# Moving copy-outs, head steps and one row fetch in the mixer stage of a hybrid diffusion layer

## The chip, the core and the metric

The kernel runs on one core of a Trainium2 chip. The core has a matrix engine (TensorE, in the profile PE, with its weight loads as PEld), a vector engine (VectorE, DVE), a scalar engine (ScalarE, ACT), GpSimd (POOL) and a queue engine (SyncE, SP) that here only issues transfers. Each works through its own list of instructions in the order in which the program left them, and waits for the others by semaphores. Sixteen DMA engines, shared by all queues, move data between main memory and the on-chip buffers. The metric is the device time of one execution in microseconds (us), lower is better.

## The reference

One layer of a diffusion backbone over 256 latent and 256 context tokens, D_MODEL = 2048, in float32. What matters here:

```python
qa, ka, va, qb, kb, vb, rb, lrf, lrb, gate_a, gate_b = jnp.split(h @ w_in, offs, axis=-1)
gf = log_sigmoid(lrf @ w_gate_f + b_gate_f) / GLA_GATE_NORM        # and gb, per GLA head
...
o_attn = windowed_attention(qa, ka, va, cka, cva, attn_sink)
o_gla = latent_gla(qb, kb, vb, gf, gb, sf, sb)                     # 4 heads, two directions
y_att = o_attn @ w_attn_o
y_gla = (rms_norm(o_gla, gla_norm) * silu(rb)) @ w_gla_o
x = x + mod_x[2] * ((sigmoid(gate_a) * y_att + sigmoid(gate_b) * y_gla) @ w_out)
x = x + mod_x[5] * conv_ffn(modulate(x, ...), w_up, conv_w, conv_b, w_down)
```

`gate_a` and `gate_b` are two products of the normalised latent tokens with 2048 columns of `w_in` each. The four heads of the gated linear attention (GLA) need, for each head, a decay computed from low-rank columns and then a 256 x 256 matrix built up in eight levels of doubling block size.

## The kernel before

Every large product streams a float32 weight in tiles of 256 rows by 512 columns (512 KB). A tile is loaded by SP into a buffer called `raw` (line 105, a pool `wr` of seven, which the copies to memory and the token rows share), ACT rounds it to `whi` (line 220), DVE subtracts to get `wlo` (line 221), both in pools of three, and PE multiplies both with the high and low halves of the activations `h..hi`, `h..lo` into banks `acc` (line 84; four banks). Splits are put ahead of other work of their engine where the scheduler can.

`proj_nat` and `proj_T` run such a product for 512 columns over eight tiles. Ahead of each tile they call `tick()`, and in its middle `midway()`; both advance whatever runs beside the product:

- `later`: functions handed to `defer(n, fn)`, called n ticks later;
- `beside = [generator, rate, 0.0]`: `aside()` adds the rate at every tick and every midway and takes one step of the generator per whole unit;
- `bg_steps` and `bg_rate`: one background step per whole unit at each tick. Each step (`mod_latent`) loads 512 KB of `w_modT` into a `raw` buffer and runs one custom DVE instruction on it (line 403). There are 100 steps, to be used up before the output product.

The stage of interest comes after the first products. Blocks in order: KB (`kb_block`, keys of heads 2 and 3, latent and context tokens, eight tiles of 24 matmuls), KA (`kept(KA, ...)`, the same size), then eight gate blocks `gate_blocks` of 512 columns for the latent tokens only: GA0 to GA3 and GB0 to GB3, eight tiles of 12 matmuls each. Then `all_values` runs 17 steps of `inner` (line 84, banks `pg`) and `outer`.

`kept` copies the finished banks to a `raw` buffer on ACT (line 1010) and sends it to memory by a DMA issued from ACT's own queue (line 1012), to be read again much later. `evac` is called as soon as the block's matmuls have been written down.

Beside these blocks run the four GLA heads, one generator `along()` of 16 places per head. `gate(h)` makes one of four pieces of the decay (matmul `pz`, ACT, DVE, POOL), `gla_A` is the levels: per level up to four exponentials on ACT (lines 892, 893, 899, 900), two products on DVE (894, 901), up to four additions on DVE on `segs` (903 to 906), eight small matmuls `pa` (line 96), a predicated copy (875); then the end of a head (lines 917 to 921, splits by lines 62 and 63, and the last `pa` products). `with_gla` gives head 0 to KB and head 1 to KA at rate 1.0 (16 calls of `aside`, 16 places), head 2 to GA0-GA3 and head 3 to GB0-GB3 at rate 0.3 (64 calls each); what is left of a head when its blocks are written down is run at once.

In GB3 the rows of the context and latent tokens are fetched again: `fetch(step)` loads, for two steps at a time, 1 MB `rows` (a broadcast of `drows`) and for each step 512 KB of `x` and `ctx` into a `raw` buffer; `natural(step)` scales, splits and writes them to memory (`dh`) and then fetches the next step. `fetch(0)` comes at GB3's first tick, `natural(0)` two and `natural(1)` five ticks later. A `rows` tile takes a large buffer of pool `M` (16 buffers) that something else has to leave first.

Of the kernel before, what the change touches and what calls it, by code (L numbers as in the profile page):

```python
# [32 lines left out]
def layer_kernel(ctx, tc, A, out):  # L33
# [115 lines left out]
    def defer(n, fn):  # L149

        later.append([n, fn])
# [808 lines left out]
            gates[h] = next(it), it  # L960
        next(gates[h][1])

    def with_gla(h, kb, block, rate=1.0):
        own = []

        def level():
            if not own:
                own.append(gla_A(h, kb, qbt, *gates[h][0]))
            next(own[0], None)

        this, following = lambda: gate(h), lambda: gate(h + 1)
        places = {i: [this] for i in ((0, 1, 2, 3) if h == 0 else (0, 1))}
        for i in (4, 6, 7, 8, 9, 10, 11, 12) if h == 0 else (2, 4, 5, 7, 8, 10, 11, 12):
            places[i] = [level]
        places.update({13: [level], 14: [following], 15: [level]})
        places.setdefault(13 if h == 0 else 9, []).append(following)

        def along():
            for i in range(16):
                for fn in places.get(i, ()):  # L980
                    fn()
                yield

        beside[:] = [along(), rate, 0.0]
        v = block()
        for _ in beside[0]:
            pass
        beside.clear()
        return v

    def kb_block():
        kb = []

        def evac(i, b):
            if not kb:
                kb.append(M("kb1", [P, 4, 512]))
            S.activation(kb[0][:, i, :], b, AF.Copy)

        proj_T(w_in, KB + 512, ALL, [h_both], evac, by_tile=True)
        return kb[0]  # L1000

    def kept(c0, name, lhs, by_tile=False):
        n = len(lhs)
        d = dram.tile([P, n, 512], F32, name=name)
        raw = []

        def evac(i, b):
            if i % 2 == 0:
                raw[:] = [wr.tile([P, 2, 512], F32, name="raw", tag="raw")]
            S.activation(raw[0][:, i % 2, :], b, AF.Copy)  # L1010
            if i % 2:
                nc.scalar.dma_start(d[:, i - 1:i + 1, :], raw[0])

        proj_nat(w_in, 0, c0, ALL, lhs, evac, by_tile=by_tile)
        return d
# [4 lines left out]
    def fetch(step):  # L1020
        if step >= KT:
            return
        kp = step % (KT // 2)
        raw = wr.tile([P, 4, T], F32, name="raw", tag="raw")
        if step >= KT // 2:
            load(raw, dh[kp])
            fetched[step] = raw
            return
        if kp % 2 == 0:
            r = M("rows", [P, 2, 4, T])  # L1030
            load(r, drows[kp:kp + 2].rearrange("k r d -> (k r d)").partition_broadcast(P))
            rows[step], rows[step + 1] = r[:, 0], r[:, 1]
        for s, src in enumerate((A["x"], A["ctx"])):
            load(raw[:, 2 * s:2 * s + 2, :], src[0][:, kp * T:(kp + 1) * T].rearrange("(t p) d -> p t d", p=P))
        fetched[step] = raw

    defer(2, send_rows)
    kb1 = with_gla(0, kbt, kb_block)
    dka = with_gla(1, kbt, lambda: kept(KA, "dka", h_xc, True))
    gate_a, gate_b = [], []  # L1040

    def gate_blocks(c0, name, to):
        for j in range(4):
            if c0 == GB and j == 3:
                defer(0, lambda: fetch(0))
                defer(2, lambda: natural(0))
                defer(5, lambda: natural(1))
            to.append(kept(c0 + j * 512, f"{name}{j}", h_x))

    def natural(step):  # L1050
        raw = fetched.pop(step)
        e = step % 2
        if step >= KT // 2:
            a = S.activation(hh[e][:, 1], raw, AF.Copy).ins
            in_order(last_hi[0], a)
            in_order(last[0], a)
            a = V.tensor_tensor(hl[e][:, 1], raw, hh[e][:, 1].bitcast(F32), op=ALU.subtract).ins
            in_order(last_lo[0], a)
            fetch(step + 1)
            return  # L1060
        r = rows.pop(step)
        for i in range(4):
            a = V.scalar_tensor_tensor(raw[:, i, :], raw[:, i, :], rcol[:, i:i + 1], r[:, i // 2, :],
                                       op0=ALU.mult, op1=ALU.mult).ins
            in_order(last_lo[0], a)
            in_order(last[0], a)
        for s in range(2):
            x_ = raw[:, 2 * s:2 * s + 2, :]
            V.tensor_tensor(x_, x_, r[:, 2 + s:3 + s, :].to_broadcast([P, 2, T]), op=ALU.add)
        split(hh[e][:, 1], hl[e][:, 1], raw)  # L1070
        nc.scalar.dma_start(dh[step], raw)
        fetch(step + 1)

    bg_rate[:] = [0.3, 0.0]
    with_gla(2, kb1, lambda: gate_blocks(GA, "da", gate_a), 0.3)
    with_gla(3, kb1, lambda: gate_blocks(GB, "db", gate_b), 0.3)
    bg_rate[:] = [0.0, 0.0]

    att = M("att", [P, 2048])
# [65 lines left out]
    def all_values():  # L1145
        last_kp = KT // 2 - 1
        banks = []

        def inner(step):
            e = step % 2  # L1150
            ax, ac = pair_x[step // (KT // 2)], pair_c[step // (KT // 2)]
            hn = (hh[e][:, 1], hl[e][:, 1])
            gb = [bank("pg", (P, 2, T), side=True) for _ in range(2)]
            for n, (x_, y_) in enumerate(((0, 0), (0, 1), (1, 0))):
                for k in range(2):
                    for s in range(4):
                        if s < 2:
                            m_ = ax[:, y_, :, 2 * s:2 * s + 2, :].rearrange("p h b c -> p h (b c)")
                        else:
                            m_ = ac[:, y_, :, s - 2, :]  # L1160
                        mm(gb[k], hn[x_][:, s, k * P:(k + 1) * P], m_, start=(n == 0 and s == 0),
                           stop=(n == 2 and s == 3))
            for k in range(2):
                split(hh[2 + e][:, 1, 2 * k:2 * k + 2, :], hl[2 + e][:, 1, 2 * k:2 * k + 2, :], gb[k])

        def outer(step, i, w):
            kp, pair, e = step % (KT // 2), step // (KT // 2), step % 2
            if kp + i == 0:
                banks[:] = [acc.tile([P, 512], F32, name="acc", tag="acc") for _ in range(4)]
            hi, lo = w  # L1170
            gs = [g[2 + e][:, 1].rearrange("p (k h) t -> p k h t", h=2) for g in (hh, hl)]

            def part0(t):
                for k in range(2):
                    for x_ in range(2):
                        mm(banks[2 * i + t], gs[x_][:, k, i, t * P:(t + 1) * P], hi[:, k, :],
                           start=(kp == 0 and k + x_ == 0), stop=False)

            def part1(t):
                for k in range(2):  # L1180
                    mm(banks[2 * i + t], gs[0][:, k, i, t * P:(t + 1) * P], lo[:, k, :], start=False,
                       stop=(kp == last_kp and k == 1))

            if kp == last_kp:
                for t in range(2):
                    part0(t)
                    part1(t)
                    out_pair(pair, i, t, banks[2 * i + t])
                return
            for part in (part0, part1):  # L1190
                for t in range(2):
                    part(t)

        def out_pair(pair, i, t, po):
            if len(og) <= pair:
                og.append(M("og", [P, 2, 2, 512]))
            S.activation(og[pair][:, i, t, :], po, AF.Copy)
            junk = W2("fb", "junk", [P, 512])
            S.activation(junk, po, AF.Square, accum_out=ssg[:, 2 * pair + i, t:t + 1])

        for step in range(KT + 1):
            if step in (1, KT // 2):
                bg_rate[:] = [0.3 if step == 1 else 0.7, 0.0]
            if 0 < step < KT - 1:
                natural(step + 1)
            if step < KT:
                inner(step)
            if step:
                pair, kp = divmod(step - 1, KT // 2)
                for i in range(2):  # L1210
                    tick()
                    c0 = VB + (2 * pair + i) * 512
                    outer(step - 1, i, wsplit(w_in[kp * 2 * P:(kp + 1) * 2 * P, c0:c0 + 512]))
# [134 lines left out]
            pass  # L1348
        beside.clear()

    bg_rate[0] = 0.75
    for j in range(1, 4):
        rb_block(j)

# [276 lines left out]
```

## Time and profile before

| what | value |
|---|---|
| median of three runs | 1969.03 us (1967.55 to 1970.83) |
| the profiled execution | 1970.05 us, its span 1968.3 us |
| KB and KA | 197.8 to 315.7 us of the span |
| GA0 to GA3 | 315.7 to 429.8 us |
| GB0 to GB3 | 429.8 to 544.8 us |
| all_values | 544.8 to about 711 us |

The block boundaries are the starts of the first matmul of a block in the timeline of PE. Times inside the profile count from the start of the span; 1.75 us of the profiled execution lie around it. "Busy" counts instructions in work; the idle time in front of a group is put down to what ended it (the releaser). A row of the stretches view gives, for a stretch, the busy time of each engine with its instruction count, then the clock granted to PE, the share of time that the DMA engines were busy, and GB/s.

### The profile page before, as it was taken

To read this page: it belongs to the slowest core of one execution; us is meant where nothing else is said; L and a number is where in the kernel's file an instruction comes from. 1 tells how busy PE (TensorE), PEld (TensorE's weight loads), DVE (VectorE), ACT (ScalarE), POOL (GpSimd) and SP (SyncE) were. 2 spreads that over 40 slices of the span, in tenths; PEclk is the share of its full clock that TensorE was granted. 3 is DMA by queue.
4 is the path that set the end of the run, shared out by engine and by line. 5 is a ranking of instruction groups with operands and counts; after the bars stand their busy time and mean duration, and the time that the engine had idled before them with its cause. 6 is when DMAs were issued, how large, how long until landed. Compare 5 with 4: busy or idle time off the path is not lost.

```text
span 1968.3 us, 26419 instructions
## 1 busy us (share of the span) xinstructions
PE 1928.2 (98%) x9858; PEld 1599.9 (81%) x9858; DVE 1446.6 (73%) x2241; ACT 1007.6 (51%) x1469; POOL 49.6 (3%) x81
## 2 busy tenths in 40 slices
PE   8999999999899999999999999999999999999999
PEld 6678787777688888778888888888888888888887
DVE  5756776858677858889888867898886545777754
ACT  5223666555344455666444445765555334555533
POOL 0010110000100000000000000000000000000000
PEclk9999999999999999999999999999999999999999
DMA  9984323757786765446999988688886566666663
GB/s 396 412 303 130 98 62 132 233 204 243 239 279 214 231 221 149 119 141 198 317 378 365 338 290 274 192 276 280 265 285 225 192 195 185 191 191 190 194 211 113
DMA packets 193376, 450.24 MB, mean 229 GB/s; under 512 B 13648, under 2 KB 18000, under 8 KB 187360
## 3 DMA queue, kind: packets, MB, share of 16 engines
q1 hardware_dynamic: 187568, 428.13, 65.3%
q0 software_dynamic: 2912, 10.82, 1.6%
q10 hardware_dynamic: 2768, 9.61, 1.2%
q8 instruction: 77, 1.26, 0.3%
q14 instruction: 51, 0.42, 0.1%
HBM read 435.86 MB, written 12.65 MB: 228 GB/s over the span
## 4 chain that ended last, share of the span: by engine, by line
PE 92%; DMA 4%; DVE 2%; ACT 1%; issue 0%; ACTq 0%; SPq 0%; DVEq 0%
PE acc L84 68%; PE accs L84 12%; PE pg L84 4%; PE pa L96 2%; DMA raw<-in_w_in 2%; PE poa L96 1%; PE pS L96 1%; DMA mraw<-in_w_mod 1%; PE pm L96 1%; PE ptp L99 1%; DMA xr<-in_ctxT 1%; DVE wlo L221 1%; ACT whi L220 1%; ACT raw L1010 0%; DMA db<-raw 0%
## 5 line engine op out<-in xcount | busy, mean ns | idle before, releaser
L221 DVE TENSOR_TENSOR wlo<-raw,whi 128x1024 fp32r<-128x1024 f32 x568 | 692.5, 1224 | 365.5 <-ACT whi L220 355.4
L220 ACT ACTIVATE whi<-raw 128x1024 fp32r<-128x1024 f32 x568 | 600.0, 1060 | 700.4 <-PE acc L84 416.8
L84 PE MATMUL accs<-h,whi 128*128 128x512 f32 x704 | 244.5, 392 | 0.0
L84 PE MATMUL acc<-h,whi 128*128 128x512 f32 x640 | 222.3, 392 | 0.0
L84 PE MATMUL accs<-h,wlo 128*128 128x256 f32 x704 | 196.0, 278 | 0.0
L84 PE MATMUL acc<-h,wlo 128*128 128x256 f32 x640 | 178.1, 278 | 0.0
L84 PEld LDWEIGHTS accs<-h,whi 128*128 128x128 f32 x704 | 131.8, 187 | 29.9
L84 PEld LDWEIGHTS acc<-h,whi 128*128 128x128 f32 x640 | 119.8, 187 | 27.0
L84 PE MATMUL acc<-whi,ah 128*128 128x512 f32 x352 | 137.0, 389 | 0.0
L84 PE MATMUL acc<-whi,al 128*128 128x512 f32 x352 | 137.0, 389 | 0.0
L84 PEld LDWEIGHTS accs<-h,wlo 128*128 128x128 f32 x704 | 132.5, 188 | 0.0
L84 PEld LDWEIGHTS acc<-h,wlo 128*128 128x128 f32 x640 | 120.5, 188 | 0.1
L84 PE MATMUL acc<-whi,h0hi 128*128 128x512 f32 x192 | 79.3, 413 | 23.0 <-ACT whi L220 23.0
L84 PE MATMUL acc<-whi,h2hi 128*128 128x512 f32 x256 | 101.5, 396 | 0.0
L84 PE MATMUL acc<-whi,h3hi 128*128 128x512 f32 x256 | 100.5, 393 | 0.8 <-ACT whi L220 0.8
L84 PE MATMUL acc<-whi,th 128*128 128x512 f32 x256 | 100.5, 393 | 0.0
L84 PE MATMUL acc<-whi,h3lo 128*128 128x512 f32 x256 | 99.8, 390 | 0.0
L84 PE MATMUL acc<-whi,h2lo 128*128 128x512 f32 x256 | 99.8, 390 | 0.0
L84 PE MATMUL acc<-whi,tl 128*128 128x512 f32 x256 | 99.7, 389 | 0.0
L84 PE MATMUL acc<-wlo,ah 128*128 128x512 f32 x352 | 94.2, 389 | 0.0
L403 DVE CUSTOM_DVE_ANT_0 raw<-raw,csrow,pack 128x1024 f32<-128x1024 f32 x64 | 81.8, 1279 | 0.0
L84 PE MATMUL acc<-whi,h0lo 128*128 128x512 f32 x192 | 78.0, 406 | 0.0
(389 smaller groups left out, 3589.1 us busy)
## 6 DMA issues: line engine op xcount, KB each, us to landing
raw<-in_w_in SPq DMA_DIRECT2D x204, 512.0 KB, 4.5
raw<-in_w_up SPq DMA_DIRECT2D x176, 512.0 KB, 4.5
raw<-in_w_modT SPq DMA_DIRECT2D x128, 512.0 KB, 5.0
raw<-in_w_down SPq DMA_DIRECT2D x88, 512.0 KB, 4.0
mraw<-in_w_mod SPq DMA_DIRECT2D x32, 1024.0 KB, 13.9
raw<-in_w_attn_o SPq DMA_DIRECT2D x32, 512.0 KB, 5.7
raw<-in_w_gla_o SPq DMA_DIRECT2D x32, 512.0 KB, 6.0
raw<-in_w_out SPq DMA_DIRECT2D x32, 512.0 KB, 5.9
```

What stands on the lines that cost most here:

```text
L84: r = pe_seq(PE.matmul(*a, **k))
L96: return pe_seq(after(PE.matmul(*a, **k)))
L99: return pe_seq(after(PE.transpose(*a)))
L220: j = S.activation(hi[:, 0:n, :], raw[:, 0:n, :], AF.Copy).ins
L221: i = V.tensor_tensor(lo[:, 0:n, :], raw[:, 0:n, :], hi[:, 0:n, :].bitcast(F32), op=ALU.subtract).ins
L403: i0 = V.tensor_tensor_reduce(out=raws[i], in0=raws[i], in1=row[0], scale=1.0, scalar=d if h else bmod[:, b0:b0 + 1], op0=ALU.mult, op1=AL ...
```

## The change

- `kept.evac`: for blocks with two banks (all gate blocks, not KA) the two copies and the DMA are deferred by two ticks, into the next block, or into `all_values` for GB3.
- The four heads become one generator `all_heads` of 64 places. It runs at 0.85 in KB and KA and at 0.32 in all gate blocks, without being emptied between blocks.
- `natural(1)` no longer fetches step 2; `all_values` does so at its start.
- The background rate is 0.35 for 0.3 in the gate blocks, 0.4 for 0.3 in the first half of `all_values`, 0.72 for 0.75 in the last products before the merge.

```diff
+    kbs = [kbt, kbt]
-    def with_gla(h, kb, block, rate=1.0):
+    def head_steps(h):
         own = []
         def level():
             if not own:
-                own.append(gla_A(h, kb, qbt, *gates[h][0]))
+                own.append(gla_A(h, kbs[h], qbt, *gates[h][0]))
             next(own[0], None)
...
-        def along():
-            for i in range(16):
-                for fn in places.get(i, ()):
-                    fn()
-                yield
-
-        beside[:] = [along(), rate, 0.0]
-        v = block()
-        for _ in beside[0]:
-            pass
-        beside.clear()
-        return v
+        for i in range(16):
+            for fn in places.get(i, ()):
+                fn()
+            yield
+
+    def all_heads():
+        for h in range(4):
+            yield from head_steps(h)
...
-        def evac(i, b):
+        def copy_out(i, b):
             if i % 2 == 0:
                 raw[:] = [wr.tile([P, 2, 512], F32, name="raw", tag="raw")]
             S.activation(raw[0][:, i % 2, :], b, AF.Copy)
             if i % 2:
                 nc.scalar.dma_start(d[:, i - 1:i + 1, :], raw[0])
+
+        def evac(i, b):
+            if n > 2:
+                copy_out(i, b)
+            else:
+                defer(2, lambda: copy_out(i, b))
...
-    kb1 = with_gla(0, kbt, kb_block)
-    dka = with_gla(1, kbt, lambda: kept(KA, "dka", h_xc, True))
+    beside[:] = [all_heads(), 0.85, 0.0]
+    kbs.extend([kb_block()] * 2)
+    dka = kept(KA, "dka", h_xc, True)
...
-        fetch(step + 1)
-    bg_rate[:] = [0.3, 0.0]
-    with_gla(2, kb1, lambda: gate_blocks(GA, "da", gate_a), 0.3)
-    with_gla(3, kb1, lambda: gate_blocks(GB, "db", gate_b), 0.3)
+        if step != 1:
+            fetch(step + 1)
+    bg_rate[:] = [0.35, 0.0]
+    beside[1] = 0.32
+    gate_blocks(GA, "da", gate_a)
+    gate_blocks(GB, "db", gate_b)
+    for _ in beside[0]:
+        pass
+    beside.clear()
...
+        fetch(2)
         for step in range(KT + 1):
             if step in (1, KT // 2):
-                bg_rate[:] = [0.3 if step == 1 else 0.7, 0.0]
+                bg_rate[:] = [0.4 if step == 1 else 0.7, 0.0]
...
-    bg_rate[0] = 0.75
+    bg_rate[0] = 0.72
```

How the change moves instructions, at two places. First ACT, where block GA0 ends and GA1 begins; `whi<-raw` is the split of a weight tile, `raw<-acc` the copy-out of the two banks, `da<-raw` its DMA, the others belong to a head. Before, the rows from the last exponential of GA0 on; the three splits at the end are GA1's first three tiles:

```order
L893 ACTIVATE q_3109<-segs 128x64x4
L1010 ACTIVATE raw<-acc 128x512 x2
L1012 DMA da_2859<-raw 128x1024
L899 ACTIVATE k_3113<-segs 128x64x4
L900 ACTIVATE k_3113<-segs 128x64x4
L220 ACTIVATE whi<-raw 128x1024 x3
```

In the changed kernel the first split row here is that of GA1's second tile (its first stands some rows further up), and the last one that of GA1's third tile:

```order
L220 ACTIVATE whi<-raw 128x1024
L817 ACTIVATE ge<-ge,ones 128x512
L892 ACTIVATE q_3126<-segs 128x256
L892 ACTIVATE q_3191<-segs 128x128x2
L62 ACTIVATE ac<-pa 128x512
L899 ACTIVATE k_3195<-segs 128x128x2
L1007 ACTIVATE raw<-acc 128x512 x2
L892 ACTIVATE q_3245<-segs 128x64x4
L1009 DMA da_2758<-raw 128x1024
L220 ACTIVATE whi<-raw 128x1024
```

The copies and their DMA moved behind the splits of the next block's first two tiles; ahead of the third split stand now the copies, the DMA and one exponential. At the other five boundaries from GA1 to GB3 the copies stand in the same way between the second and the third split.

Second SP, the loads around the start of GB3. `in_w_in` are weight tiles, `in_w_modT` background loads, `rows<-drows` a row fetch, `in_x` and `in_ctx` the tokens. Before, the first row of three weight tiles is the middle of GB2, the second its last three, and the row of two is GB3's first two; the row fetch is that of steps 2 and 3, the tokens are those of steps 0 and 1:

```order
L105 DMA raw<-in_w_in 128x2x512 x3
L105 DMA raw<-in_w_modT 128x1024
L105 DMA raw<-in_w_in 128x2x512 x3
L105 DMA rows<-drows 128x2048
L105 DMA raw<-in_x 128x2x256
L105 DMA raw<-in_ctx 128x2x256
L105 DMA raw<-in_w_modT 128x1024
L105 DMA raw<-in_w_in 128x2x512 x2
L105 DMA raw<-in_x 128x2x256
L105 DMA raw<-in_ctx 128x2x256
```

After, the first row is GB2's last two tiles, the two single weight tiles are GB3's first and second, the row of two at the end its third and fourth; the row fetch is again that of steps 2 and 3:

```order
L105 DMA raw<-in_w_in 128x2x512 x2
L105 DMA raw<-in_x 128x2x256
L105 DMA raw<-in_ctx 128x2x256
L105 DMA raw<-in_w_in 128x2x512
L105 DMA raw<-in_w_modT 128x1024
L105 DMA raw<-in_w_in 128x2x512
L105 DMA rows<-drows 128x2048
L105 DMA raw<-in_x 128x2x256
L105 DMA raw<-in_ctx 128x2x256
L105 DMA raw<-in_w_in 128x2x512 x2
```

The row fetch moved behind GB3's first two weight tiles and the tokens of step 0. The buffer that it waits for is another one too: before it was the `segs` of head 3, read last by line 920; now it is the buffer of the queries `qb`, read last by line 921 of the same head, one DVE instruction later. The tokens of step 2 moved from behind GB3's fifth weight tile to behind its eighth.

## The prediction

> **What bounds the kernel now.** I read the page's busy totals first, then PE's waits in the stage that changes, then that stage cut at the block boundaries.
>
> ```profile
> PE 1928.2 (98%) x9858; PEld 1599.9 (81%) x9858; DVE 1446.6 (73%) x2241; ACT 1007.6 (51%) x1469; POOL 49.6 (3%) x81
> ```
>
> PE is the bound, and nothing here takes products away from it. What can be won is idle time of PE and time in which it runs slowly. The waits of PE in the gate blocks (315 to 545 us: engine and line, what it waited for, us in total, times, longest):
>
> ```profile
> PE acc L84 <- ACT whi L220: 23.8, 9, 8.3
> PE acc L84 <- DVE wlo L221: 0.4, 1, 0.4
> ```
>
> Nearly all is one wait, for ACT's split. Seven of its nine times are the starts of GA0 to GB2, some 2 us each, one, of 8.25 us, is the start of GB3, and the ninth, 0.82 us, lies within GB3. The stretches of the eight blocks follow (us; PE, PEld, DVE, ACT, POOL busy with counts; granted clock; DMA share; GB/s):
>
> ```profile
> 315.74:343.50 27.76, 25.88 (x114) 21.42 (x114) 17.81 (x26) 15.81 (x25) 2.15 (x2) 0.94 0.60 202
> 343.50:370.46 26.96, 24.77 (x120) 20.63 (x120) 24.84 (x44) 14.36 (x26) 0.00 (x0) 1.00 0.70 225
> 370.46:400.17 29.71, 27.53 (x129) 22.85 (x129) 20.40 (x32) 16.17 (x27) 1.00 (x1) 0.94 0.59 195
> 400.17:429.77 29.60, 27.36 (x113) 22.34 (x113) 15.19 (x19) 13.62 (x20) 0.97 (x1) 0.94 0.59 197
> 429.77:455.98 26.21, 24.31 (x114) 20.26 (x114) 21.21 (x32) 15.83 (x25) 2.86 (x3) 1.00 0.82 299
> 455.98:483.66 27.68, 25.07 (x120) 20.55 (x120) 23.65 (x42) 14.92 (x26) 0.00 (x0) 1.00 0.62 200
> 483.66:517.60 33.94, 25.68 (x128) 21.52 (x128) 23.43 (x37) 16.17 (x26) 4.08 (x11) 0.95 0.63 214
> 517.60:544.80 27.20, 26.37 (x120) 21.80 (x121) 21.01 (x29) 9.93 (x10) 3.49 (x5) 0.94 0.87 289
> sum 229.06, PE 206.97 PEld 171.37 DVE 167.54 ACT 116.82 POOL 14.55; mean PE 25.87 PEld 21.42 DVE 20.94 ACT 14.60 POOL 1.82
> ```
>
> The stage lasts 229.06 us. How short could it be? Pieces of the chain of waits give the price of each kind of PE work (start, us, engine and line, count):
>
> ```profile
> 556.52 5.44 PE acc L84 x24
> 495.76 0.89 PE pa L96 x8
> 305.02 0.23 PE pz L96
> 251.92 3.45 PE pa L96 x16
> 307.97 2.87 PE pa L96 x24
> ```
>
> A weight matmul undisturbed takes 5.44 / 24 = 0.227 us, so 8 blocks x 8 tiles x 12 = 768 of them take 174.1 us. Two heads have 7 levels with 8 small products each beyond the first, and four more groups: I count 144 at 0.89 / 8 = 0.111 us, 16.0 us; six `pz` at 0.23, 1.4 us; and the ends of heads 2 and 3, priced like those of heads 0 and 1, 3.45 and 2.87 us. That is 197.8 us. **The excess is 229.1 - 197.8 = 31.3 us**, the most that the eight blocks can give.
>
> Where does it lie? First the idle time: 23.8 + 0.4, less the 2.15 before GA0 that stand ahead of the stretch, is 22.1 us. A boundary looks like this on PE and on ACT (start, us, instruction, in brackets the idle time before it):
>
> ```profile
> 315.74 0.63 PE L84 MATMUL acc<-whi,h0hi 128*128 128x512 f32 x1 [2.15 <-ACT whi L220]
> 370.48 0.73 PE L84 MATMUL acc<-whi,h0hi 128*128 128x512 f32 x1 [2.18 <-ACT whi L220]
> 517.61 0.80 PE L84 MATMUL acc<-whi,h0hi 128*128 128x512 f32 x1 [8.25 <-ACT whi L220]
> 367.88 1.08 ACT L1010 ACTIVATE raw<-acc 128x512 f32<-128x512 f32 x2 [0.94 <-PE acc L84]
> 369.00 0.33 ACTq L1012 DMA_DIRECT2D da<-raw  x1
> 369.37 2.95 ACT L220 ACTIVATE whi<-raw 128x1024 fp32r<-128x1024 f32 x3 [0.40 <-ACT raw L1010]
> ```
>
> ACT stands in order: it waits for the block's last matmul, copies (1.08), issues the DMA (0.33), and only then splits the next block's first tile (2.95 / 3 = 0.98). That is the wait of 2.18 us.
>
> Second, slow clock. In five of the eight rows the granted clock is 0.94 or 0.95. In GB2's the low clock falls into the idle 8.25 us at its end; for three others the chain shows what it costs:
>
> ```profile
> 370.48 3.68 PE acc L84 x8
> 315.74 6.40 PE acc L84 x20
> 400.19 4.58 PE acc L84 x12
> ```
>
> Eight matmuls behind the wait take 3.68 instead of 8 x 0.227 = 1.81 us, 1.87 more; 6.40 for 20 and 4.58 for 12 exceed their clean time by the same 1.9. The fourth such stretch is the last row's, behind 517.61, taken at the same. So 4 x 1.86 = 7.4 us. The 1.8 us left are not placed.
>
> **The change part by part.** *Copies two ticks later.* By the order rows the first two splits of the next block stand ahead of the copies, and only the third behind. When the last matmul ends, PE has two tiles ready, 5.44 us of work. ACT needs 1.08 + 0.33 + at most 0.4 for the exponential + 1.06 for the split, 2.9 us; with a stray pair of head operations 4.2. Cover holds, so the six 2-us waits from GA1 to GB2, GB3's share and that of the value stage go. The cover is gone if ACT takes over 5.4 us here; then each boundary costs the surplus. The banks are no problem: a block has two of four and the next use of the same two is a block (over 24 us) later.
>
> KA has four banks and its copies aren't moved, so GA0's 2.15 us and its 1.87 us of slow start stay. The excess to be had falls to 31.3 - 1.87 = 29.4 us. ACT also gains one exponential ahead of GA0's first split there: 0.4 us lost.
>
> *The row fetch and GB3.* The long wait is made on SP and by transfers:
>
> ```profile
> SPq L105 <- ACT q L920: 14.6, 1, 14.6
> 503.39 0.34 SPq L105 DMA_DIRECT2D rows<-drows  x1
> 516.50 1.06 ACT L220 ACTIVATE whi<-raw 128x1024 fp32r<-128x1024 f32 x1 [6.47 <-DMA raw<-in_w_in]
> ```
>
> SP stood 14.6 us at the row fetch, until head 3 left its large buffer; GB3's first weight tile, three transfers behind it, was split only at 516.50. After the change that tile and the next stand ahead of the fetch. The head also gets through earlier: 27 of 64 head steps lie in KB and KA (0.85 x 32) and the other 37 at 0.32 a call take 115 of the gate blocks' 128 calls, with line 921, for which SP now waits, at about call 109, in GB2's seventh tile; before, it came in the eighth. So some 2 us before GB3 begins, SP is free. I take the 8.25 us and the slow stretch behind it as gone.
>
> What is late next is GB3's fifth tile: its buffer is the one from which GB2's copy is written. Counted from GB3's start, copy 1.08, issue 0.33, write, then load, ACT's split 1.06 and DVE's 1.22. Write and load are these:
>
> ```profile
> DMA to landing us min/median/max: 2.6/2.6/8.1
> raw<-in_w_in SPq DMA_DIRECT2D x204, 512.0 KB, 4.5
> L221 DVE TENSOR_TENSOR wlo<-raw,whi 128x1024 fp32r<-128x1024 f32 x568 | 692.5, 1224 | 365.5 <-ACT whi L220 355.4
> ```
>
> With the copy's write at 2.6 to 8.1 us and the load at 4.5, the tile is ready at 8.2 + 2.6 = 10.8 to 8.2 + 8.1 = 16.3 us; PE wants it at 4 x 2.72 + about 3 x 0.89 = 13.6. So from nothing to 2.7 us late; as this block is thick with transfers I charge the upper end, **2.5**. In the other blocks this buffer goes to the seventh tile, wanted at some 18 us, and nothing is late.
>
> *More work beside the gate blocks.* DVE has 167.5 us in them. Five head steps come in (37 for 32), each at most (167.5 - 64 x 1.22 - 19 x 1.28) / 32 = 2.0 us, together 8 to 10; 0.05 x 64 = 3.2 more background steps at 1.28 add 4.1:
>
> ```profile
> L403 DVE CUSTOM_DVE_ANT_0 raw<-raw,csrow,pack 128x1024 f32<-128x1024 f32 x64 | 81.8, 1279 | 0.0
> ```
>
> So DVE has 181 of some 205 us, 88%, where it had 73%. The nearest row is GA1's, 24.84 of 26.96, 92%, and its only idle time on PE was the boundary's. From nothing to 5 us over all blocks; I charge **2.5**. The PE work of the moved head steps is only shifted. KB and KA are five steps lighter; their waits of PE for the heads, 1.2 us in two times, can go. I credit 1.0:
>
> ```profile
> PE pa L96 <- DVE k L901: 1.2, 2, 1.1
> ```
>
> *The value stage and the tail.* GB3's copies, the tokens of step 2 and 1.4 more background steps (1.8 us of DVE) go to the value stage, where PE never idles and DVE is at 77%:
>
> ```profile
> 560.00:711.00 151.00, 151.00 (x675) 124.99 (x674) 115.60 (x175) 66.94 (x98) 0.58 (x1) 1.00 0.73 234
> ```
>
> I cost that, and the lower rate of 0.72 at the end, at nothing: the spare DVE time covers it, and uncovered it would be at most the 1.8 us. The tokens are issued some 10 us ahead of the stage and used about 16 us after its start.
>
> **Sum.** 29.4 - 2.5 - 2.5 - 0.4 + 1.0 = 25.0 us. The profiled execution took 1970.05, so 1945.05; it lay 1.0 above the median, which makes **1944.0**. Its own range: all 31.3 and KB's 1.2 gained is 1936.5; the three charges doubled with no gain in KB leaves 18.6 gained, 1950.5.
>
> **The rivals.** *The last block stays bound by transfers (0.16).* Between its first load and the value stage's first, SP sends about 10.5 MB: eight weight tiles (4), three background loads (1.5), two row fetches (2), the tokens of three steps (1.5), the finished tokens of two (1) and a copy (0.5). In 25 us that is 420 GB/s; the row at 515 us shows 399:
>
> ```profile
> 515.00:520.00 5.00, 2.39 (x6) 1.91 (x7) 1.65 (x2) 2.12 (x2) 4.83 (x12) 0.50 1.06 399
> ```
>
> What speaks against it is that some of these now start 14 us before the block. If wait and slow stretch stay, 8.25 + 1.87 - 2.5 charged = 7.6 come back: 1951.6.
>
> *DVE becomes the bound (0.12).* If it can be kept busy to only 85% (GB1's row is at 23.65 / 27.68), 181 / 0.85 = 213 us; the stage falls from 229.1 to 213 and the rest adds 0.6 of gain: 1952.4, with waits of PE for line 221.
>
> *The slow stretches are no echo of the waits (0.05).* Behind the waits at 343.52 and 429.79, as long as the others, the clock stayed at 1.00, so a 2-us wait doesn't always cost it. If something else sets it, 3 x 1.86 = 5.6 us stay: 1949.6. [...]
>
> *Slower (0.04).* The copy's buffer is returned two ticks later in each block; if its write is slow, the block's seventh tile is late. It is ready at 8.2 us plus the write and wanted at 18; for the 25 us to be lost over seven blocks, each must lose 3.6, so from a write of 13.4 us on the kernel is slower. The longest seen is 8.1. At 19 us: 9 x 7 = 63 less 25, 2007.
>
> *Given back (0.05).* The earlier transfers or the 1.8 us of DVE open waits of the same size in the value stage: 1969. Its row above, with no idle time at all and 234 GB/s, speaks against it. That the change doesn't do what it says is ruled out by the order rows: the splits do stand ahead of the copies.
>
> **How the numbers follow.** The forecast has 0.58. Nearly all of it, the first three rivals and two of them partly together (to about 1957) make 0.85 between 1936.5 and 1957; no bound of a charge reaches further. A measurement of this kernel can tell about 0.2%, 3.9 us. Faster: 0.58 + 0.16 + 0.12 + 0.05 = 0.91; same: the given-back case, 0.05; slower 0.04.
>
> **What would show it.** The 2-us waits of PE for `whi` at the starts of GA1 to GB2 are gone and GA0's remains; the clock is 1.00 from GA1 on; SP's long wait is at line 921's buffer and ends before GB3's first tile is needed; the stage takes about 205 us; DVE is near 88%. I am wrong if waits of about 1 us for `wlo` are spread over the blocks, if GB3's start still waits over 5 us, or if the value stage's PE row falls below full.

## The result, and the profile after

The changed kernel takes **1942.81 us** (median of four runs, 1942.35 to 1944.42); the kernel before takes 1968.99 us beside it. The ratio is **0.9868, 95% interval 0.9851 to 0.9885**, so it is faster by 26 us. The forecast was 1944.0 us in a range of 1936.5 to 1957.

First PE's waits of the changed kernel from 195 to 560 us (engine and line, what it waited for, us in total, times, longest), and each of those for the split in its place in the timeline:

```profile
PE acc L84 <- ACT whi L220: 5.1, 3, 2.7
PE pg L84 <- DVE h2lo L63: 0.2, 1, 0.2
```

```profile
307.95 0.50 PE L84 MATMUL acc<-whi,h0hi 128*128 128x512 f32 x1 [2.15 <-ACT whi L220]
501.97 0.50 PE L84 MATMUL acc<-whi,h2hi 128*128 128x512 f32 x1 [0.28 <-ACT whi L220]
510.36 0.50 PE L84 MATMUL acc<-whi,h3hi 128*128 128x512 f32 x1 [2.65 <-ACT whi L220]
```

Of nine waits for the split, 23.8 us, three are left. GA0's is the same 2.15 us as before; the other two lie in GB3. Then the eight gate blocks as stretches (us; PE, PEld, DVE, ACT, POOL busy; granted clock; DMA share; GB/s), cut at the blocks' new starts:

```profile
307.95:336.04 28.09, 28.06 (x146) 23.80 (x146) 23.60 (x33) 18.55 (x30) 2.12 (x2) 1.00 0.69 237
336.04:360.06 24.02, 24.02 (x115) 20.18 (x114) 18.96 (x28) 16.49 (x26) 2.67 (x2) 1.00 0.72 224
360.06:384.77 24.71, 24.71 (x122) 20.89 (x121) 24.32 (x45) 16.16 (x29) 0.00 (x0) 1.00 0.75 251
384.77:413.65 28.88, 28.88 (x146) 24.65 (x145) 26.50 (x44) 18.42 (x32) 2.73 (x2) 1.00 0.81 240
413.65:437.78 24.13, 24.13 (x116) 20.26 (x115) 18.53 (x26) 16.43 (x24) 2.47 (x3) 1.00 0.80 272
437.78:462.36 24.58, 24.58 (x124) 20.79 (x122) 24.11 (x44) 14.50 (x27) 0.00 (x0) 1.00 0.82 260
462.36:487.75 25.39, 25.39 (x130) 21.59 (x129) 23.87 (x39) 15.49 (x27) 1.65 (x3) 1.00 0.78 266
487.75:517.54 29.79, 26.85 (x121) 21.87 (x120) 20.53 (x29) 10.16 (x12) 6.33 (x12) 0.94 0.90 306
sum 209.59, PE 206.62 PEld 174.03 DVE 180.44 ACT 126.20 POOL 17.97; mean PE 25.83 PEld 21.75 DVE 22.55 ACT 15.78 POOL 2.25
```

From GA0 to GB2 PE is busy from end to end and the clock is 1.00. DVE has 24.32 of 24.71 us in GA2 and PE doesn't wait for it. Nearly all that is left lies in GB3. SP's wait at the row fetch of steps 2 and 3 is now this:

```profile
SPq L105 <- DVE q L921: 3.8, 1, 3.8
```

It ends at 481.80 us, 6 us before GB3 begins; before, it took 14.6 us and ended at 503.39, with GB3's first two weight tiles still behind it in the queue.

From KB's start to the first product of the value stage the time went from 545.0 - 197.8 = 347.2 to 517.5 - 197.7 = 319.8 us, 27.4 less. The span fell from 1968.3 to 1941.1, 27.2 less. So next to nothing was won or lost elsewhere.

A boundary now looks like this on ACT, at the start of GA2 (360.06):

```profile
359.90 1.07 ACT L1007 ACTIVATE raw<-acc 128x512 f32<-128x512 f32 x2
361.00 0.33 ACTq L1009 DMA_DIRECT2D da<-raw  x1
362.97 0.42 ACT L892 ACTIVATE q<-segs 128x256 f32<-128x256 f32 x1 [2.00 <-PE pa L96]
363.29 1.04 ACT L220 ACTIVATE whi<-raw 128x1024 fp32r<-128x1024 f32 x1
```

The copies still run the moment the banks are finished, but PE works meanwhile on two tiles that were split ahead of them. The third split ends at 364.3, 4.3 us into the block; PE needs it at 5.4 us and 0.9 more for a head's products.

### The profile page after: what moved, and what is told of

Read it like the earlier page. It is cut to its first block, busy times and chain, and to the rows that moved or that the text cites. A ratio compares the mean times of both kernels' runs of the same rounds, so it can differ in the third digit from the quotient of the medians.

```text
span 1941.1 us, 26437 instructions
## 1 busy us (share of the span) xinstructions
PE 1920.8 (99%) x9858; PEld 1596.2 (82%) x9858; DVE 1446.7 (75%) x2241; ACT 1007.9 (52%) x1469; POOL 50.9 (3%) x81
## 4 chain that ended last, share of the span: by engine, by line
PE 94%; DMA 4%; ACT 1%; DVE 1%; issue 0%; ACTq 0%; SPq 0%
PE acc L84 70%; PE accs L84 13%; PE pg L84 4%; PE pa L96 2%; DMA raw<-in_w_in 1%; PE poa L96 1%; PE pS L96 1%; DMA mraw<-in_w_mod 1%; PE pm L96 1%; DMA xr<-in_ctxT 1%; PE ptp L99 1%; DMA db<-raw 0%; DMA dh<-raw 0%; PE pto L99 0%; DMA pack<-in_k_pack 0%; DVE wlo L221 0%
## 5 line engine op out<-in xcount | busy, mean ns | idle before, releaser
L84 PEld LDWEIGHTS acc<-whi,ah 128*128 128x128 f32 x352 | 66.1, 188 | 13.8
```

The lines of the kernel that those rows point to most:

```text
L84: r = pe_seq(PE.matmul(*a, **k))
```

## The experiments

Eleven runs in three sets; those of a set ran on one chip beside the kernel before (1971.2, 1971.1 and 1971.6 us).

| run | median us | ratio to before, interval |
|---|---|---|
| p1_no_deferral | 1968.95 | 0.9994 (0.9981 to 1.0007) |
| p2_deferral_alone | 1945.26 | 0.9872 (0.9854 to 0.9890) |
| p3_tokens_as_before | 1943.40 | 0.9861 (0.9843 to 0.9880) |
| p4_heads_as_before | 1947.34 | 0.9885 (0.9862 to 0.9907) |
| q1_one_tick | 1947.59 | 0.9881 (0.9864 to 0.9898) |
| q2_more_background | 1946.31 | 0.9873 (0.9857 to 0.9890) |
| q3_gb2_copy_later | 1943.41 | 0.9862 (0.9846 to 0.9878) |
| q4_ka_split | 1941.04 | 0.9852 (0.9830 to 0.9875) |
| r1_changed_again | 1942.87 | 0.9857 (0.9843 to 0.9872) |
| r2_ka_split_no_background_in_gb3 | 1942.34 | 0.9855 (0.9838 to 0.9871) |
| r3_same_and_gb2_copy_later | 1939.97 | 0.9842 (0.9827 to 0.9857) |

### Which part of the change brings it

**The deferral undone**, heads, rates and fetches as changed:

```diff
-                defer(2, lambda: copy_out(i, b))
+                copy_out(i, b)
```

> The changed kernel with one part undone: the gate blocks' copies and their DMA stand again right behind the block. Theory (the copies are the main part, and they also order SP's queue: with the copy's buffer taken early the row fetch stands again ahead of GB3's first tile): the six waits of PE of about 2 us at GA1 to GB2 are back (12.6 us), some of them with a slow stretch of 1.9 us, GB3 starts with a wait of 2 to 8 us; about 1964 us (1958 to 1968). Rival (the heads that run over and the later token fetch are worth a good part by themselves): the waits at GA1 to GB2 are back without more, GB3's is short; about 1956.

Measured 1968.95 us, no different from before. Waits of PE and of SP, and a later row of PE's timeline:

```profile
PE acc L84 <- ACT whi L220: 19.6, 8, 6.1
```

```profile
SPq L105 <- DVE q L921: 14.7, 1, 14.7
```

```profile
569.53 1.22 PE L84 MATMUL pg<-ax,h1hi 128*128 128x512 f32 x2 [3.53 <-DVE h2lo L63]
```

Five of the six boundaries wait again, GB3 waits 6.1 us, and SP stands 14.7 us at the row fetch, as long as before, although the head is earlier. A new wait of 3.53 us in the value stage brings the time just above the theory's range. The earlier head frees SP no sooner here because the buffer is now line 921's: the fetch goes out 19.9 us into GB2, where it went out 19.7 us into it before. The rival falls: without the deferral, heads and fetch bring nothing that can be measured.

**The deferral alone**, in the kernel before (the same `copy_out` and `evac` as in the diff of the change, and nothing else of it).

> The kernel before with the deferral of the gate blocks' copies alone; heads, rates and fetches as before. Theory: six waits of 2 us and their slow stretches go, and GB3's 8.25 us shrink to about 3, since its first two tiles now stand ahead of the row fetch; KB's waits of 1.2 us stay: about 1945 us (1943 to 1948). Rival (GB3's wait is the late head's: line 920 comes as late as before, so SP stands as long): GB3's wait and its slow stretch stay, about 1952.

Measured 1945.26 us, as the theory says. Why SP stands shorter here is seen in the order of its queue. Around the row fetch of steps 2 and 3 it reads as follows in this run, where the row of two ahead of the fetch is GB3's first two weight tiles:

```
L105 DMA raw<-in_x 128x2x256
L105 DMA raw<-in_ctx 128x2x256
L105 DMA raw<-in_w_modT 128x1024
L105 DMA raw<-in_w_in 128x2x512 x2
L105 DMA rows<-drows 128x2048
L105 DMA raw<-in_x 128x2x256
L105 DMA raw<-in_ctx 128x2x256
```

and so in the run without the deferral, where the row of two ahead of it is GB2's last two, and GB3's first comes behind:

```
L105 DMA raw<-in_w_in 128x2x512 x2
L105 DMA rows<-drows 128x2048
L105 DMA raw<-in_x 128x2x256
L105 DMA raw<-in_ctx 128x2x256
L105 DMA raw<-in_w_in 128x2x512
```

The later copy alone moves the fetch, as both pairs of kernels show; that it does so because copies and loads take their buffers from one pool is read from the program. SP's wait is 5.2 us for 14.6:

```profile
SPq L105 <- ACT q L920: 5.2, 1, 5.2
```

**The tokens of step 2 as before:**

```diff
-        if step != 1:
-            fetch(step + 1)
+        fetch(step + 1)
...
-        fetch(2)
```

> The changed kernel with one part undone: the tokens and rows of step 2 are fetched by the second token step of GB3 again. Theory (only the order of a few transfers in GB3 moves): 1943 to 1945.5 us, PE's waits in GB3 between 2 and 5 us. Rival (the fetch is what freed GB3): waits of over 7 us in GB3, about 1949 or more.

Measured 1943.40 us, with 2.5 us of waits in GB3. The fetch is worth nothing that can be measured.

**The heads as before**, one generator for each, emptied at the end of its blocks:

```diff
-    beside[:] = [all_heads(), 0.85, 0.0]
-    kbs.extend([kb_block()] * 2)
-    dka = kept(KA, "dka", h_xc, True)
+    kb1 = with_gla(0, kbt, kb_block)
+    dka = with_gla(1, kbt, lambda: kept(KA, "dka", h_xc, True))
...
-    beside[1] = 0.32
-    gate_blocks(GA, "da", gate_a)
-    gate_blocks(GB, "db", gate_b)
+    with_gla(2, kb1, lambda: gate_blocks(GA, "da", gate_a), 0.3)
+    with_gla(3, kb1, lambda: gate_blocks(GB, "db", gate_b), 0.3)
```

> The changed kernel with one part undone: one generator per head again, emptied at the end of its blocks, rates 1.0 and 0.3; copies and fetches as changed. Theory: only what KB and KA gained comes back, 2.2 us: 1945 us (1943.5 to 1947), boundaries from GA1 to GB3 without a wait. Rival (the steps that run over keep DVE and ACT free at the boundaries): waits of about 1 us at GA1, GB0 and in GB3, 1949 or more.

Measured 1947.34 us, just above the theory's range. KB's waits of 1.2 us are back and the boundaries have none, but GB3's third tile waits:

```profile
499.52 0.57 PE L84 MATMUL acc<-whi,h1hi 128*128 128x512 f32 x1 [4.48 <-ACT whi L220]
```

SP stands 7.2 us at the row fetch, for the later line 921. So the later token fetch, by which that buffer is taken, needs the earlier heads. The heads without it are worth little: p3, which has them, is 1.9 us below p2 on the same chip, and KB's waits are 1.2 of that. The background rates differ between these two as well, and no run undid them alone, so their share stays open.

### How much cover a boundary needs

**One tick for two:**

```diff
-                defer(2, lambda: copy_out(i, b))
+                defer(1, lambda: copy_out(i, b))
```

> The changed kernel with the gate blocks' copies deferred by one tick instead of two. ACT then has one tile of cover (2.7 us of PE, 3.6 where a head's products stand in it) for 1.08 + 0.33 + 1.06 = 2.5 us of copies, DMA and split, and what a head has there. Theory (cover decides): waits of PE of 0 to 0.5 us at the second tile of a block, GB3's first waits come earlier since the row fetch stands ahead of its second tile (2 to 6 us in GB3): 1945 us (1943 to 1949). Rival (one tile's cover isn't enough, as the split waits for the DMA's issue too): over 1 us at each of six blocks, 1950 or more.

Measured 1947.59 us, inside the theory's range, but not by its mechanism alone: two blocks of six wait at their second tile, 1.45 us each and not 0.5 at most, the others not at all. ACT and PE at the start of GA2 (360.94):

```profile
360.69 1.09 ACT L1007 ACTIVATE raw<-acc 128x512 f32<-128x512 f32 x2 [0.82 <-PE acc L84]
361.81 0.33 ACTq L1009 DMA_DIRECT2D da<-raw  x1
363.85 0.42 ACT L892 ACTIVATE q<-segs 128x256 f32<-128x256 f32 x1 [2.07 <-PE pa L96]
...
365.09 2.94 ACT L220 ACTIVATE whi<-raw 128x1024 fp32r<-128x1024 f32 x3
```

```profile
366.18 0.50 PE L84 MATMUL acc<-whi,h0hi 128*128 128x512 f32 x1 [1.45 <-ACT whi L220]
```

Copies and DMA (1.09 and 0.33 us) fit under one tile, 2.7 us of PE. What doesn't are a head's four exponentials that wait for PE behind them and stand ahead of the second split. The second tick pays for these.

### Does DVE have room

**A background rate of 0.5 for 0.35 in the gate blocks** (one number in `bg_rate`).

> The changed kernel with a background rate of 0.5 for 0.35 in the gate blocks: 9.6 more steps there, 12.3 us of DVE and 4.8 MB, fewer of them later. DVE goes from 180.4 to about 193 us of 209.6, 92%. Theory (DVE still has room, since splits go first): waits of PE for line 221 of under 2 us in all, GB3 1 to 3 us worse by its transfers: 1944 us (1942 to 1947). Rival (DVE is close to being the bound at 86% already): waits for line 221 of 5 us and more, 1949 or later.

Measured 1946.31 us. PE waits nowhere for line 221, and GA1 to GB2 last as long as in the changed kernel. GB3's waits, 2.8 us, are the changed kernel's 2.9. Of the 3.5 us between the profiled spans, 1.8 are waits for DVE's splits at the start of the value stage (2.0 for 0.2), and 1.3 are a slow start of GA0 (29.36 us for 28.09; its first eight matmuls take 3.01 us for 2.14), which the edit doesn't explain, as the last section shows. So DVE wasn't about to become the bound in the gate blocks.

### What is left in GB3

**GB2's copy seven ticks later**, so that no weight tile of GB3 is loaded into its buffer:

```diff
-                defer(2, lambda: copy_out(i, b))
+                defer(7 if name == "db2" else 2, lambda: copy_out(i, b))
```

> The changed kernel with GB2's copy alone deferred by seven ticks instead of two, so that no weight tile of GB3 is loaded into the buffer from which that copy is written. Theory (the 8.16 us of that write hold GB3's fifth tile, and through it its seventh): GB3's waits of 0.28 and 2.65 us and the slow clock behind them go, 1938.5 us (1937 to 1941). Rival (GB3 is late because its transfers crowd each other, some 10 MB in 30 us): waits of 2 us or more stay in GB3, 1942 or more.

In the changed kernel the chain through GB3 runs over that write (start, us, what; lines between left out):

```profile
488.67 8.16 DMA db<-raw
...
496.89 3.86 DMA raw<-in_w_in
...
504.94 6.19 DMA raw<-in_w_in
```

The first load is that of GB3's fifth tile, the second that of its eighth. With the copy later, GB3 has no wait at all and ends 4.5 us earlier in the profile (513.0 for 517.5), as the theory says. But the time stays at 1943.41 us, as the rival says. The timeline and the chain of this run show where it comes back:

```profile
532.57 0.76 PE L84 MATMUL pg<-ax,h0hi 128*128 128x512 f32 x2 [3.04 <-ACT h0hi L62]
```

```profile
513.44 8.15 DMA dh<-raw
...
522.11 4.99 DMA raw<-in_w_in
```

Another write of 8 us, of finished tokens, holds the buffer of a weight tile of the value stage; that stage is 4.4 us longer (from its first product to the last of these products 169.6 us, 165.2 in the changed kernel). The theory was right on where PE waits and wrong on the time, the rival the other way round. It looks as if the buffer sets where PE waits and the sum of the transfers how long; the second half isn't shown.

**KA's last two banks copied two ticks later:**

```diff
-            if n > 2:
+            if i < n - 2:
```

> The changed kernel with KA's third and fourth bank copied two ticks later too (the first two are copied at once, since GA0 needs them). GA0's first split then stands ahead of the last two copies. Theory: GA0's wait of 2.15 us falls to 0 to 0.5, nothing else moves: 1941 us (1939.5 to 1943). Rival (GA0's first bank is free only when its copy is read out, so PE waits for line 1007 instead): a wait of 1 us or more for the copy, 1942 to 1944.

Measured 1941.04 us (1939.61 to 1944.70, so its runs overlap those of the changed kernel). PE's waits in the stage, in one line:

```profile
PE acc L84 <- ACT whi L220: 2.8, 1, 2.8
```

GA0 starts without a wait, 2.1 us earlier, and PE doesn't wait for the two early copies either; the one wait that is left is GB3's.

**Both, with fewer bytes in GB3.** The first run has the edit above and no background in GB3, the second GB2's copy seven ticks later as well; the changed kernel ran once more beside them.

```diff
-    bg_rate[:] = [0.35, 0.0]
+    bg_rate[:] = [0.45, 0.0]
...
+                bg_rate[:] = [0.0, 0.0]
                 defer(0, lambda: fetch(0))
```

> The changed kernel once more, beside the two below on the same chip. 1942.8 us, GA0's wait of 2.15 us and about 2.9 us of waits in GB3.

> The changed kernel with KA's last two banks copied two ticks later, no background step in GB3 (three loads of 512 KB and 3.8 us of DVE less there) and a rate of 0.45 for 0.35 in the seven blocks before it. Theory (GB3 and the start of the value stage are limited by what they transfer together, so that moving a wait doesn't help and moving bytes does): GA0's wait is gone (2.15), GB3's 2.65 and its slow clock shrink to under 1 us, and nothing is late in the value stage: 1937 us (1935.5 to 1939.5). Rival (DVE at 98% in GA2 and GB1 has no room for 0.1 more): waits for line 221 in the seven blocks, 1941 or more.

> As the run before, and GB2's copy seven ticks later as well. Theory (bytes count, not the buffer): no better than the run before, 1937 us (1935.5 to 1940). Rival (with fewer bytes the buffer of GB2's copy is the last wait in GB3): 1 to 2 us better than the run before.

The changed kernel came to 1942.87 us again. The first combination, 1942.34, missed its range: GB3 has no wait (24.66 us, the shortest seen), but the value stage waits for DVE, whose split there stands behind a weight tile's `wlo`, a background step of 1.28 us and a token row:

```profile
520.57 1.22 PE L84 MATMUL pg<-ax,h1hi 128*128 128x512 f32 x2 [3.46 <-DVE h2lo L63]
```

The second, **1939.97 us (1937.61 to 1941.80), is the best kernel here**, 2.9 us below the changed kernel beside it (1942.38 to 1943.46); the runs don't overlap, though the two intervals to the kernel before do. Its runs overlap a little with r2's, and with q4's. It lies inside the theory's range, but the rival named the difference to r2 better: 2.4 us. It has the same GB3 and 2.5 us of waits in the value stage instead of 3.5 and a slow stretch (granted clock 0.63 from 518 to 523 us). So less in GB3 alone isn't enough, against the theory, and what the last copy's buffer adds could be a matter of how the order falls out. In the seven blocks of the first combination PE waits for line 221 once, 0.39 us in GA3, where DVE is busy 28.54 of 29.56 us and the subtraction stands behind seven instructions of a head. In the changed kernel's GA2 DVE is busy 24.32 of 24.71 us without such a wait, so the order of DVE's work counts there, and not its busy share alone.

## Why the prediction was right

**The size.** The forecast gain was 25.0 us, the measured one 26.2 by medians and 27.2 by the profiled spans. The terms erred in both directions:

- *The six waits of 2 us* went, all of them, by the mechanism given; p2 shows that the deferral alone does it, and p1 that without it five of the six stay.
- *GA0's wait* stayed at 2.15 us, as forecast. *Its slow start* of 1.87 us was kept in the sum and was not there in the profiled execution: eight matmuls took 2.14 us from 307.95 on. That is luck, as the last section shows. 1.9 us better.
- *GB3* was charged 2.5 us; its waits are 2.9, and behind 510.36 two tiles take 517.54 - 510.36 = 7.2 us for 5.4, so 4.7 in all. The write was taken at its upper end of 8.1 and took 8.16 us. The step that was too small is what follows: the fifth tile was only 0.28 late, but the seventh is loaded into the fifth's buffer, and its load of 6 us for 4.5 made it 2.65 late; the low clock behind that wait (0.94 over the block) is the one place from GA1 on where the clock isn't 1.00. 2.2 us worse.
- *DVE crowding* was charged 2.5 and cost nothing. DVE's time, forecast at 181 us, is 180.4; at 24.32 of 24.71 us in GA2 PE didn't wait. 2.5 us better.
- *KB and KA* were credited 1.0 and charged 0.4. The waits of 1.2 us are gone. The two blocks take 110.2 us for 117.9; some 5.6 of that is work of the heads (48 small products and a `pz`) that moved to the gate blocks, and 2.1 is won. 1.5 us better.
- Of the 1.8 us that had no place, which the sum counted as gain, about 1.5 are still there: 209.6 - 197.8 - 5.6 of moved work - 4.7 in GB3. 1.5 us worse.

25.0 + 1.9 - 2.2 + 2.5 + 1.5 - 1.5 = 27.2 us, the difference of the spans. The errors cancel in part, so the time came out closer than its terms; that part is luck. The 205 us forecast for the stage left out the 5.6 us of moved work; without them the 209.6 are 204.0.

**The reasons.** Two reasons were given for GB3's start: that its first two tiles stand ahead of the fetch, and "The head also gets through earlier". The first is enough. p1 has the earlier head and SP stands 14.7 us; p2 has the late head and SP stands 5.2. The place of the row fetch in SP's queue does it, and that comes from the deferral. The earlier head is needed only since the later token fetch put line 921's buffer in the way (p4). With both, line 921 came in GB2's seventh tile as forecast, and SP was free 6 us before GB3, not 2.

**The rivals.** That GB3 stays bound by transfers came true in part: 4.7 of its 10 us stayed, and q3, r2 and r3 show GB3's wait gone and the value stage longer by about half of it or more. DVE as the bound: no (q2), and with a rate of 0.45 one wait of 0.39 us (r2). The slow clock from another cause: with the waits gone the rows from GA1 to GB2 are at 1.00, and the 5.6 us were won. With the waits back in p1, the granted clock is 0.94 over GA2 and over GB1, and 1.00 over GA1 and GA3, which start behind such a wait too. So the slow stretches came with the waits, though not with every wait. Slower through late tiles: only GB3, where the buffer is used earliest, had any. Given back later: the value stage takes the same 165.2 us as before, from its first to its last product of this kind.

What stays open: why the value stage's waits in r3 are shorter than in r2 wasn't taken apart.

## What to carry to other kernels

Here a copy that had to wait for the end of a block delayed everything behind it on ACT, and PE with it by 1.9 to 2.2 us at each of six boundaries. So put as many pieces of the next block's preparation ahead of such an instruction as cover its own time and whatever else the engine has to wait for there (one tile wasn't enough here, two were). Taking a buffer later from a shared pool can also move the loads around it, here a blocking fetch out of the way of two weight tiles (SP's wait at it fell from 14.6 to 5.2 us in p2), so read the order of the load queue before and after. Where a stretch is as thick with transfers as GB3 (DMA share 0.90), a wait that is taken away at one buffer can turn up in the stage behind it (3.04 us in q3), and moving bytes out of the stretch alone didn't end that (3.46 us in r2); so look at the stage behind it too.

## What the runs showed of the hardware

The slow clock behind a short wait isn't fixed by the wait. The same kernel with the same 2.15 us of idle time in front of GA0 started at full speed in one execution (307.95, clock 1.00 over 4 us, eight matmuls in 2.14 us) and slow in the other (r1):

```profile
308.14:312.00 3.86, 3.86 (x10) 3.10 (x11) 3.86 (x5) 1.98 (x3) 0.00 (x0) 0.56 0.60 232
```

Here the granted clock is 0.56 over the first 3.86 us of GA0, and the eight matmuls take 3.53. Ten of the profiles here have this wait of 2.15 us, and three of them start GA0 slow: the kernel before (clock 0.57 over 4 us), q2 (eight matmuls in 3.01 us) and r1. What decides between a fast and a slow start isn't shown. One such wait is therefore worth its length here, and in these three profiles 1.3 to 1.9 us more.
